# Input tiles and weight blocks in a fixed alternating order at the start of a hybrid decoder kernel

## The chip, the cores and the metric

The kernel runs on all eight cores of one Trainium2 chip. Each core has TensorE (matmuls), ScalarE (ACT), VectorE (DVE), GpSimd (POOL), SyncE (SP) and 16 DMA engines; the page gives each DMA queue's share of them (39.3% and 14.4% for the two large queues of the kernel before). Cores 0 to 3 are die 0 and cores 4 to 7 are die 1. The metric is the device time of the slowest core, in microseconds (us). Executions come in a fast and a slow state (four of the kernel before in one set took 781.88, 781.89, 782.39 and 916.83 us); only fast ones are compared by time here, or the cores of an undisturbed die. A ratio is the mean time of one kernel's fast runs over that of the other kernel's fast runs of the same rounds, so it is not quite the ratio of the medians that are quoted beside it.

## The reference, cut to what matters

```python
u = rmsnorm(x, norm_g)                 # 2048 prompt rows and 16 sample rows a core, 1024 wide
proj = u @ w_in                        # 1024 x 8704: cut into 68 weight blocks of 128 columns
lx, lg, sb, scg, sh, sg, q, qg, mg = split(proj)
# branch A: conv(lx) -> RG-LRU gates -> scan over time, times silu(lg), @ lru_wo
# branch B: conv(scg * sh) * sb * silu(sg), @ sconv_wo
# branch C: softmax(q k^T) v * silu(qg), @ xa_wo; k, v = rmsnorm(mem) @ xa_wk, xa_wv
y = (sigmoid(mg_a) * z_a + sigmoid(mg_b) * z_b + sigmoid(mg_c) * z_c) @ w_out
return rmsnorm(x + y)                  # and the new states; inputs and outputs are float32
```

## The kernel before

The program describes tasks and lets a list scheduler put them in order at build time. The scheduler holds a simple model of every engine and of the DMA queues; it decides nothing on the chip. What it fixes is the order of instructions in each engine's queue. At run time semaphores make an engine wait where data are not there (TensorE 9.3 us for `w_in` in 20:70 us of the kernel before, core 0), and the traces show the queues served in their order: in the kernel before ACT stood 10.6 us before one eviction with the squares of three tiles behind it. **If data come later than the model thought, an engine stands before the one instruction that waits, with ready work behind it.**

```python
# in Graph.run: the model that plans the order
for r, t in lst:
    if r <= m + 0.4:                       # choose by priority among what starts this soon
        k = t.prio
...
if t.dma is not None:
    q, o = ("sw", "hw") if t.eng == "pool" else ("hw", "sw")
    a, n = max(dmafree[q], end + 0.8), t.dma[1] / 250e3      # bytes at 250 GB/s
    both = min(2 * n, max(0.0, dmafree[o] - a))
    dmafree[q] = a + n + both / 2
    fin = dmafree[q] + 1.3
```

The input phase takes 17 tiles of up to 128 rows (512 KB each): load on the SP queue, sum of squares on ACT, reciprocal root on POOL, scaling on DVE or POOL, eight transposes on TensorE, a copy with the norm weights on DVE. Two memory tiles follow, then the state of the samples (`sin`), which is loaded into space that the squares use before.

```python
def p0(ti, src, nr, dst, gcols, tdst, prio):
    x_, xn_, ps = Handle(xring), Handle(xnring), Handle(PS)      # xring: 9 buffers
    G.dma("sp", [(lambda: x_.ap[0:nr, :], src)], nr * 4096, [], [x_.tok], prio, None)
    G.act(... AF.Square ... accum_out=stat ...)
    rstd(ti, nr, prio)
    ... scale; G.pe([tr(kc) for kc in range(KC)], ...); G.dve(... mult by gcols ...)

def wload(ap, prio):                        # one block: 256 KB in bfloat16, on the POOL queue
    ...
    if state["nw"] >= 2:
        G.after(t, t_rs[min(16, state["nw"] + 1)])     # only an order in the plan

def unit(lhs, nk, rhs, u, reads, prio, hold=()):    # 688 columns, two PSUM banks of 344
    ps = Handle(PS)
    ...
    G.pe([mm(k, b) for k in range(nk) for b in range(2)], ...)   # 16 matmuls 128x344

for hd in range(4):
    step(heads_q, hd)
step(branch_A_lg, 0); step(branch_B_sg, 0); step(branch_A_lx, 0)
kv(pos)                                     # memory K/V
for n in range(NCH + 1):                    # 6 chunks of branches A and B
    ...
    if n < 4:
        step(attend, n, d=14)
```

The softmax here doesn't subtract the row's maximum and nothing guards it: scores larger than these inputs give would overflow.

## Time and profile before

| | |
|---|---|
| time | 781.89 us median of 3 (781.88 to 916.83; the last is slow) |
| cores of the profiled run | 776.0 to 782.0 us, mean 778.1 |
| TensorE busy | 726.6 us, 93% of the span |
| TensorE idle in 0:70 us | 30.4 us |

The page's picture in 40 slices (19.5 us each) of the kernel before: a digit is the busy share in tenths; the second row is the clock that TensorE was granted.

```profile
PE   2579998999999998999999999999999999999995
...
PEclk9979998999999999999999999999999999999998
```

TensorE is the engine that sets the time, and more than half of its idle time (30.4 of 55.4 us) lies in the first 70 us. The table by stretches of core 0 shows where; the columns are the stretch, its length, then busy us and instructions of PE, PEld, DVE, ACT and POOL, then granted clock, DMA share and GB/s.

```profile
35.00:40.00 5.00, 0.00 (x0) 0.00 (x0) 1.54 (x3) 1.39 (x3) 3.56 (x6) 0.79 1.12 266
40.00:45.00 5.00, 2.87 (x11) 1.51 (x12) 0.00 (x0) 0.00 (x0) 0.00 (x0) 0.50 1.28 119
```

The timeline of TensorE, same kernel and core (start, length, what, idle time before it and its releaser), and the waits of TensorE in 20:70, name what it stood before:

```profile
24.49 4.03 PE L761 MATMUL PP<-R 128*128 128x344 bf16 x16 [1.48 <-DVE R L674]
28.36 1.50 PE L671 MATMUL PP<-R 128*128 128x128 bf16 x24
29.70 0.23 PE L627 MATMUL PP<-R 66*128 66x66 f32 x1
32.03 2.49 PE L761 MATMUL PP<-R 128*128 128x344 bf16 x16 [2.11 <-DMA R<-w_in]
34.36 0.61 PE L671 MATMUL PP<-R 128*128 128x128 bf16 x8
42.13 4.75 PE L761 MATMUL PP<-R 128*128 128x344 bf16 x16 [7.16 <-DMA R<-w_in]
```

```profile
PE PP L761 <- DMA R<-w_in: 9.3, 2, 7.2
```

A projection unit (16 matmuls) takes 2.33 us back to back later, and 4.03 and 4.75 us in the first and third unit above: most of their matmuls start 287 ns apart, where 146 ns is the interval of the later units, at a granted clock of 1.00 (60:70 us); it is called full speed here. (The granted-clock column shows only the second of these slow stretches: it reads 0.50 in 40:45, but 1.00 in 20:30, where the matmuls are 287 ns apart as well. So in this trace a 1.00 in that column at the start does not prove full speed.) The second weight block is used at 32 us and the third at 42, though the first two were issued at 2 us. Meanwhile ACT stood 10.6 us before one instruction, the eviction of the unit that waits for the third block, with the squares of three tiles behind it:

```profile
46.97 0.73 ACT L936 CAST R<-PP 128x688 bf16<-128x688 f32 x1 [10.57 <-PE PP L761]
47.59 1.06 ACT L659 ACTIVATE R<-R 128x1024 bf16<-128x1024 f32 x1
```

**A measure used below: lost TensorE time.** At a time t it is t minus the full-clock time of all matmuls started by then. Full-clock times are the start-to-start intervals that the trace shows, 146 ns for 344 columns, 216 ns for 512 and 56 ns for 128. The count runs over every TensorE record of a core, and the figures are means of the eight cores. (Two cores in each trace lack 16 to 20 of 4884 matmul records, none of them before 100 us; such a core lacks 3.5 to 4.3 us of work in the whole sum, in all kernels nearly alike. The 36 small transposes of the sample state are counted at about 100 ns each, where the trace shows 61; so all figures after them are some 1.4 us too low, in all kernels alike. They run before 70 us in `before`, e4, g1 and, in most cores, g2, and later elsewhere, so the 70 us column compares these with the others only to within 1.4 us.) Only differences between kernels are used. It takes idle gaps and slow clock together and tells at which time they came.

### The profile page before, as it was taken

The numbers are of one execution on the slowest core, as the hardware profiler recorded it, in microseconds if no ns is written. First come the engines' busy times: TensorE is split into PE (matmuls) and PEld (weight loads), VectorE is DVE, ScalarE is ACT, GpSimd is POOL, SyncE is SP. The second block draws the span as 40 slices with busy tenths as digits, with TensorE's granted clock in tenths as the row PEclk, the third lists the DMA queues.
The fourth block names the chain that finished last, engine by engine and source line by source line (L and its number), as shares of the span: only waits on it lengthen the run. The fifth ranks groups of instructions, "written<-read, shape, count | busy, mean of one in ns | idle before, by whom it ended". The sixth has DMA issues, their size and how long they took to land.

```text
span 782.0 us, 13246 instructions; the slowest of 8 cores (776.0 to 782.0 us)
## 1 busy us (share of the span) xinstructions
PE 726.6 (93%) x4884; PEld 460.6 (59%) x4884; DVE 395.2 (51%) x379; ACT 340.2 (44%) x404; POOL 247.5 (32%) x303
## 2 busy tenths in 40 slices
PE   2579998999999998999999999999999999999995
PEld 1356654655655654666666666666666666665442
DVE  3544043265684863877875874546321221223665
ACT  4442358886759658676571211121212112112332
POOL 5845000121120210212114344435464454423221
PEclk9979998999999999999999999999999999999998
DMA  8999921414242333242334595655896828226933
GB/s 223 296 92 129 117 68 15 41 15 41 28 45 25 28 34 35 28 41 24 39 31 78 81 194 88 94 110 66 111 121 73 119 28 76 23 109 215 294 141 138
DMA packets 112618, 69.47 MB, mean 89 GB/s; under 512 B 93987, under 2 KB 100213, under 8 KB 112539
## 3 DMA queue, kind: packets, MB, share of 16 engines
q0 software_dynamic: 99808, 31.60, 39.3%
q1 hardware_dynamic: 12747, 37.03, 14.4%
q8 instruction: 40, 0.66, 0.4%
q14 instruction: 23, 0.19, 0.1%
HBM read 90.53 MB, written 9.82 MB: 128 GB/s over the span
## 4 chain that ended last, share of the span: by engine, by line
PE 85%; DMA 5%; issue 2%; ACT 2%; DVE 2%; POOL 2%; SPq 0%; POOLq 0%; ACTq 0%; DVEq 0%
PE PP L761 73%; PE PP L1189 8%; DMA R<-w_in 3%; PE PP L967 2%; DMA R<-xp 1%; PE PP L901 1%; ACT R L825 1%; PE PP L959 1%; DMA R<-cv 1%; POOL R L653 1%; PE PP L1053 1%; DVE R L839 1%; ACT R L962 1%; POOL R L663 0%; DVE R L1072 0%
## 5 line engine op out<-in xcount | busy, mean ns | idle before, releaser
L761 PE MATMUL PP<-R 128*128 128x344 bf16 x4104 | 616.5, 311 | 17.2 <-DMA R<-w_in 9.3
L761 PEld LDWEIGHTS PP<-R 128*128 128x128 bf16 x4104 | 400.1, 98 | 225.9 <-issue 28.2
L133 POOL DMA_DIRECT2D R<-w_in x68 | 61.7, 910 | 293.0 <-PE PP L761 266.3
L1141 ACT ACTIVATE R<-PP 128x688 f32<-128x688 f32 x72 | 53.6, 744 | 221.8 <-PE PP L761 197.8
L1150 DVE SCALAR_TENSOR_TENSOR R<-R,PP 128x688 f32<-128x688 f32 x72 | 62.5, 871 | 157.3 <-PE PP L761 134.5
L1189 PE MATMUL PP<-R 128*128 128x512 bf16 (+1 forms) x272 | 59.0, 379 | 0.0
L1154 POOL TENSOR_TENSOR R<-R 128x688 f32<-128x688 f32 x24 | 39.3, 1642 | 33.5 <-DVE R L1150 32.5
L812 DVE SCALAR_TENSOR_TENSOR R<-R 128x2048 f32<-128x2048 f32 x18 | 42.3, 2349 | 8.1 <-ACT R L809 7.0
L1189 PEld LDWEIGHTS PP<-R 128*128 128x128 bf16 (+1 forms) x272 | 26.4, 97 | 32.2 <-issue 0.4
L1159 POOL TENSOR_TENSOR R<-R 128x688 bf16<-128x688 f32 x24 | 38.9, 1642 | 17.7 <-DVE R L1150 17.5
L1198 ACT ACTIVATE R<-R 128x1024 f32<-128x1024 f32 (+1 forms) x17 | 18.0, 1057 | 46.3 <-DVE R L1193 46.3
L867 DVE TENSOR_TENSOR R<-PP,R 128x688 f32<-128x688 f32 x18 | 15.7, 874 | 31.0 <-PE PP L761 31.0
L1193 DVE SCALAR_TENSOR_TENSOR R<-PP,R 128x1024 f32<-128x1024 f32 (+1 forms) x17 | 20.8, 1224 | 20.6 <-PE PP L1189 20.6
L825 ACT ACTIVATE R<-PP,R 128x688 f32<-128x688 f32 x36 | 27.7, 833 | 6.4 <-PE PP L761 6.4
L674 DVE TENSOR_TENSOR R<-PP,R 128x1024 bf16<-128x1024 bf16 (+1 forms) x19 | 21.6, 1171 | 17.0 <-PE PP L671 16.5
L671 PE MATMUL PP<-R 128*128 128x128 bf16 (+1 forms) x152 | 13.7, 252 | 16.5 <-DVE R L663 12.7
L873 DVE SCALAR_TENSOR_TENSOR R<-R 128x2048 f32<-128x2048 f32 x12 | 28.2, 2347 | 0.9 <-ACT R L870 0.7
L651 POOL TENSOR_SCALAR R<-R 128x1 f32<-128x1 f32 (+1 forms) x36 | 7.5, 209 | 62.5 <-ACT R L1198 44.5
L839 DVE TENSOR_TENSOR_SCAN R<-R 128x2048 f32<-128x2048 f32 x6 | 26.5, 4422 | 0.4
L975 DVE TENSOR_TENSOR R<-PP,R 128x512 f32<-128x512 f32 x16 | 10.9, 688 | 29.3 <-ACT R L973 21.4
L1055 DVE TENSOR_TENSOR R<-R,PP 128x1024 f32<-128x1024 f32 x16 | 19.5, 1216 | 11.2 <-PE PP L1053 9.4
L936 ACT CAST R<-PP 128x688 bf16<-128x688 f32 x12 | 8.8, 730 | 35.1 <-PE PP L761 33.5
(129 smaller groups left out, 587.9 us busy)
## 6 DMA issues: line engine op xcount, KB each, us to landing
R<-w_in POOLq DMA_DIRECT2D x68, 256.0 KB, 5.1
R<-xp SPq DMA_DIRECT2D x32, 512.0 KB, 9.1
R<-ck SPq DMA_DIRECT2D x16, 512.0 KB, 4.2
y_p<-R SPq DMA_DIRECT2D x16, 512.0 KB, 2.8
R<-cv POOLq DMA_DIRECT2D x16, 256.0 KB, 7.2
R<-w_out POOLq DMA_DIRECT2D x8, 256.0 KB, 6.4
R<-xa_wo POOLq DMA_DIRECT2D x14, 128.0 KB, 4.1
R<-lru_wo POOLq DMA_DIRECT2D x8, 192.0 KB, 4.6
```

The source lines that it names most:

```text
L133: eng.dma_start(out=out, in_=in_).then_inc(sems[semkey], 16)
L674: G.dve(lambda e: e.tensor_tensor(out=dst, in0=ps.ap.bitcast(BF16)[:, 0:1024].rearrange("p (k t) -> p k t", k=KC)[:, :, 0:nr], in1=gcols.u ...
L761: return lambda e: e.matmul(ps.ap[:, b * 512:b * 512 + BLK], lhs(k), rhs[:, k, c:c + BLK], start=(k == 0), stop=(k == nk - 1))
L812: G.dve(lambda e, k=k: e.scalar_tensor_tensor(out=xc[:, 0:T], in0=lxp[:, k:k + T], scalar=cw(k), in1=xc[:, 0:T], op0=ALU.mult, op1=ALU.add ...
L825: G.act(lambda e, ps=ps, dst=dst, u=u, bcol=bcol: e.activation(out=cols(dst, u), in_=pv(ps), func=AF.Tanh, scale=0.5, bias=dv[:, bcol:bcol ...
L839: G.dve(lambda e: e.tensor_tensor_scan(out=xc[:, 0:T], data0=thr[:, 0:T], data1=thi[:, 0:T], initial=0.0, op0=ALU.mult, op1=ALU.add), T, t ...
L873: G.dve(lambda e, k=k: e.scalar_tensor_tensor(out=cy[:, 0:T], in0=cinp[:, k:k + T], scalar=sw(k), in1=cy[:, 0:T], op0=ALU.mult, op1=ALU.ad ...
L1141: G.act(lambda e, ps=pg[u], th_=th_: e.activation(out=b3(th_.ap), in_=pv(ps), func=AF.Tanh, scale=0.5), UW, [pg[u].tok], [th_.tok], Px - E ...
L1150: G.dve(lambda e, zp=zp, th_=th_, dst=dst: e.scalar_tensor_tensor(out=b3(dst.ap), in0=b3(th_.ap), scalar=1.0, in1=pv(zp), op0=ALU.add, op1 ...
L1154: G.pool(lambda e, acc=acc, th_=th_: e.tensor_tensor(out=acc.ap, in0=acc.ap, in1=th_.ap, op=ALU.add), 1.6, [acc.tok, th_.tok], [acc.tok], Px)
L1159: G.pool(lambda e, acc=acc, th_=th_, u=u, j=j: e.tensor_tensor(out=mT[:, j, u * UW:(u + 1) * UW], in0=acc.ap, in1=th_.ap, op=ALU.add), 1.6 ...
L1189: return lambda e: e.matmul(ps.ap[0:nr, b * 512:(b + 1) * 512], mT[:, k, c0:c0 + nr], wo[:, k, b * 512:(b + 1) * 512], start=(k == 0), sto ...
```

## The change

Intent: each input tile from the seventh on (tile 6) waits for a weight block to land, so that blocks are no longer late behind a crowd of tiles (in the kernel before, core 0, block 1 was issued at 3.1 us and landed at 31.8, and 13 tiles landed in between); 13 blocks are requested in a fixed order, from the third on each after a tile's statistics; the two memory tiles wait for the last of them. The first units are split into two bank halves, the first of which needs only its own tiles. K/V goes behind the first chunk's gates and attention one chunk later. The scheduler's window of choice shrinks from 0.4 to 0.2 us. Cut to its core:

```diff
-                    if r <= m + 0.4:
+                    if r <= m + 0.2:
...
+            if split:
+                for b in range(2):
+                    c = u * UW + b * BLK
+                    t = G.pe([mm(k, b) for k in range(nk)], ..., own tiles of this half, ...)
+                    t.xgate = [t_tr[i] for i in range(17) if i * 128 < (u + 1) * UW] if b == 0 else []
...
+        first = [C_Q, C_Q + 128, C_Q + 256, C_Q + 384, C_LG, C_SG, C_LX, C_SB, C_LG + 128, C_SCG, C_SH, C_SG + 128, C_LX + 128]
+        pre, x_toks, w_toks = {}, [], []
         for i in range(17):
+            if i >= 6:
+                wait = [w_toks[min(i - 5, len(w_toks) - 1)]]
+            elif i >= 3:
+                wait = [x_toks[i - 3]]
+            else:
+                wait = []
...
+            x_toks.append(p0(i, src, nr, uT[...], pT[:, 0:8], t_uT[i], -100 + i, wait))
+            while len(w_toks) < len(first) and len(w_toks) <= max(1, i):
+                hw, lhs = wload(w_in_cols(first[len(w_toks)]), -100 + i)
+                ...
+                    G.after(G.tasks[-1], t_rs[i])
...
-        kv(pos)
-        pos += 10
         for n in range(NCH + 1):
...
-            if n < 4:
-                step(attend, n, d=14)
+            if n == 0:
+                kv(pos)
+                pos += 10
+            if 1 <= n < 5:
+                step(attend, n - 1, d=14)
```

(`xgate` makes the planner start a unit only after the transposes of all its tiles have been placed.)

More of the change, by code (lines that the diff above doesn't have):

```diff
@@ L181 @@
 class Task:
-    __slots__ = ("i", "eng", "dur", "fns", "reads", "writes", "prio", "hs", "tset", "npred", "succ", "pf", "dma", "preds", "start", "gate", "etset")
+    __slots__ = ("i", "eng", "dur", "fns", "reads", "writes", "prio", "hs", "tset", "npred", "succ", "pf", "dma", "preds", "start", "gate", "etset", "xgate")
 EXP = frozenset((0, 6))
@@ L248, in _add @@
         t.start = None
+        t.xgate = []
         for p in preds:
@@ L295, in _gates @@
         for t in self.tasks:
-            t.gate = []
+            t.gate = list(t.xgate)
             t.etset = None
@@ L358, in run @@
             if best is None:
-                stuck = [(t.eng, t.i, [k.name for k in t.writes], [h.ring.name for h in t.hs if h.phys is None])
-                         for c in ready.values() for t in c]
-                held = {}
-                for t in self.tasks:
-                    for h in t.hs:
-                        if h.phys is not None and h.left > 0 and t.start is None:
-                            held.setdefault((h.ring.name, h.phys), []).append((t.eng, t.i, t.prio, [k.name for k in t.reads], [k.name for k in t.writes],
-                                [(p.i, p.eng, [k.name for k in p.writes]) for p in t.preds if p.start is None][:4]))
-                raise RuntimeError(f"no task can start: {stuck[:8]} held {held}")
+                stuck = [(t.eng, t.i, [k.name for k in t.writes]) for c in ready.values() for t in c]
+                raise RuntimeError(f"no task can start: {stuck[:8]}")
             _, start, t = best
@@ L413, in run @@
                 if sem is None:
-                    h = t.hs[0]
+                    h = (t.writes or t.reads)[0].handle
                     sem = h.ring.sem + str(h.phys)
@@ L628, in params, with wload, w_in_cols, unit @@
             G.dve(lambda e: e.tensor_copy(pT[:, 16:82], h.ap[:, 0:66]), 66, [h.tok], [m_pT.t], -86)
+        def wload(ap, prio):
+            k = ap.shape[1]
+            hw = Handle(w2ring if 2 <= state["nw"] < 6 else wring)
+            G.dma("pool", [(lambda: hw.ap[:, 0:k * 128].rearrange("p (k c) -> p k c", k=k), ap)], k * 65536 * 1.18, [], [hw.tok], prio, None)
+            state["nw"] += 1
+            if "pre" in state:
+                G.after(G.tasks[-1], state["pre"])
+            return hw, (lambda i: hw.ap[:, i * 128:(i + 1) * 128])
+        def w_in_cols(c0):
+            return w_in.rearrange("(k p) c -> p k c", p=128)[:, :, c0:c0 + 128]
+        def unit(lhs, nk, rhs, u, reads, prio, hold=(), split=False):
+            ps = Handle(PS)
+            def mm(k, b):
+                c = u * UW + b * BLK
+                return lambda e: e.matmul(ps.ap[:, b * 512:b * 512 + BLK], lhs(k), rhs[:, k, c:c + BLK],
+                                          start=(k == 0), stop=(k == nk - 1))
+            if split:
+                for b in range(2):
+                    c = u * UW + b * BLK
+                    t = G.pe([mm(k, b) for k in range(nk)], nk * 0.1465, [r for r in reads if r not in t_uT] + utoks(c, c + BLK), [ps.tok],
+                             prio + 0.1 * b)
+                    t.xgate = [t_tr[i] for i in range(17) if i * 128 < (u + 1) * UW] if b == 0 else []
+            else:
+                G.pe([mm(k, b) for k in range(nk) for b in range(2)], nk * 2 * 0.1465, reads, [ps.tok], prio, hold)
+            return ps
+        def pv(ps, n=BLK):
+            return ps.ap.rearrange("p (b c) -> p b c", b=2)[:, :, 0:n]
+        def cols(arr2d, u, off=0):
+            return arr2d[:, off + u * UW: off + (u + 1) * UW].rearrange("p (b c) -> p b c", b=2)
+        def usl(u):
+            return utoks(u * UW, (u + 1) * UW)
+        def proj(c0, prio, lead=30.0, hold=((), (), ())):
+            hw, lhs = pre.pop(c0) if c0 in pre else wload(w_in_cols(c0), prio - lead)
+            return [unit(lhs, KC, uT, u, [hw.tok] + usl(u), prio + 2.4 * u, hold[u], prio < 60) for u in range(NU)]
         m_xb = [side(f"xb{i}", i * 4096, 1024, F32) for i in range(5)]
@@ L645, in build_program @@
         t_st = [m_stat.tok(f"st{i}") for i in range(40)]
-        t_rs = []
+        t_rs, t_tr = [], []
         def rstd(col, nr, prio):
@@ L654, in rstd, with p0 @@
                                [t_st[col], m_cst.t], [t_st[col]], prio))
-        def p0(ti, src, nr, dst, gcols, tdst, prio):
+        def p0(ti, src, nr, dst, gcols, tdst, prio, wait):
             x_, xn_, ps = Handle(xring), Handle(xnring), Handle(PS)
-            G.dma("sp", [(lambda: x_.ap[0:nr, :], src)], nr * 4096, [], [x_.tok], prio, None)
+            G.dma("sp", [(lambda: x_.ap[0:nr, :], src)], nr * 4096, wait, [x_.tok], prio, None)
             G.act(lambda e: e.activation(out=m_junk.ap[0:nr, :], in_=x_.ap[0:nr, :], func=AF.Square,
@@ L672, in tr @@
                                              xn_.ap[0:nr, kc * 128:(kc + 1) * 128], identb[0:nr, 0:nr])
-            G.pe([tr(kc) for kc in range(KC)], 0.65, [xn_.tok, m_identb.t], [ps.tok], prio)
+            t_tr.append(G.pe([tr(kc) for kc in range(KC)], 0.65, [xn_.tok, m_identb.t], [ps.tok], prio))
             G.dve(lambda e: e.tensor_tensor(
@@ L677, in p0 @@
                 [ps.tok, t_pg], [tdst], prio)
+            return x_.tok
+        first = [C_Q, C_Q + 128, C_Q + 256, C_Q + 384, C_LG, C_SG, C_LX, C_SB, C_LG + 128, C_SCG, C_SH, C_SG + 128, C_LX + 128]
+        pre, x_toks, w_toks = {}, [], []
         for i in range(17):
+            if i >= 6:
+                wait = [w_toks[min(i - 5, len(w_toks) - 1)]]
+            elif i >= 3:
+                wait = [x_toks[i - 3]]
+            else:
+                wait = []
             nr = 128 if i < 16 else TS
             src = xp[i * 128:(i + 1) * 128, :] if i < 16 else xs[:, :]
-            p0(i, src, nr, uT[:, :, i * 128:i * 128 + nr], pT[:, 0:8], t_uT[i], -100 + i)
+            x_toks.append(p0(i, src, nr, uT[:, :, i * 128:i * 128 + nr], pT[:, 0:8], t_uT[i], -100 + i, wait))
+            while len(w_toks) < len(first) and len(w_toks) <= max(1, i):
+                hw, lhs = wload(w_in_cols(first[len(w_toks)]), -100 + i)
+                pre[first[len(w_toks)]] = hw, lhs
+                if len(w_toks) >= 2:
+                    G.after(G.tasks[-1], t_rs[i])
+                w_toks.append(hw.tok)
+                last = G.tasks[-1]
+        state["pre"] = last
         for i in range(2):
-            p0(17 + i, memp[i * 128:(i + 1) * 128, :], 128, mnT[:, :, i * 128:(i + 1) * 128], pT[:, 8:16], t_mn[i], -80 + i)
+            p0(17 + i, memp[i * 128:(i + 1) * 128, :], 128, mnT[:, :, i * 128:(i + 1) * 128], pT[:, 8:16], t_mn[i], -80 + i, w_toks[-1:])
         params()
@@ L741, in build_program @@
               [m_pT.t, m_dv.t], [m_dv.t], -84)
-        def wload(ap, prio):
-            k = ap.shape[1]
-            hw = Handle(w2ring if 2 <= state["nw"] < 6 else wring)
-            t = G.dma("pool", [(lambda: hw.ap[:, 0:k * 128].rearrange("p (k c) -> p k c", k=k), ap)], k * 65536 * 1.18, [], [hw.tok], prio, None)
-            if state["nw"] >= 2:
-                G.after(t, t_rs[min(16, state["nw"] + 1)])
-            state["nw"] += 1
-            return hw, (lambda i: hw.ap[:, i * 128:(i + 1) * 128])
-        def w_in_cols(c0):
-            return w_in.rearrange("(k p) c -> p k c", p=128)[:, :, c0:c0 + 128]
-        def unit(lhs, nk, rhs, u, reads, prio, hold=()):
-            ps = Handle(PS)
-            def mm(k, b):
-                c = u * UW + b * BLK
-                return lambda e: e.matmul(ps.ap[:, b * 512:b * 512 + BLK], lhs(k), rhs[:, k, c:c + BLK],
-                                          start=(k == 0), stop=(k == nk - 1))
-            G.pe([mm(k, b) for k in range(nk) for b in range(2)], nk * 2 * 0.1465, reads, [ps.tok], prio, hold)
-            return ps
-        def pv(ps, n=BLK):
-            return ps.ap.rearrange("p (b c) -> p b c", b=2)[:, :, 0:n]
-        def cols(arr2d, u, off=0):
-            return arr2d[:, off + u * UW: off + (u + 1) * UW].rearrange("p (b c) -> p b c", b=2)
-        def usl(u):
-            return utoks(u * UW, (u + 1) * UW)
-        def proj(c0, prio, lead=30.0, hold=((), (), ())):
-            hw, lhs = wload(w_in_cols(c0), prio - lead)
-            return [unit(lhs, KC, uT, u, [hw.tok] + usl(u), prio + 2.4 * u, hold[u]) for u in range(NU)]
         lxp, xc, xcb, thr, thi, a2 = m_lxp.ap, m_xc.ap, m_xcb.ap, m_thr.ap, m_thi.ap, m_a2.ap
```

## The prediction

> **What bounds the kernel now.** TensorE: the page gives PE 726.6 us busy of 782.0 (93%). Most of its idle time is at the start. The table by stretches shows PE at 39.6 us busy in the first 70 us (30.4 idle), against 12 in 150:700. Part of the early busy time is slow as well: sixteen 128x344 matmuls take 4.03 to 4.75 us at 24 to 47 us and 2.33 us later; the granted clock was 0.50 at 40:45 and 0.69 at 45:50. By the PE timeline, the work done before the memory K/V matmuls start at 100.15 us is 336 projection matmuls (x 146 ns = 49.2 us), 19 tiles of transposes (0.61 each, 11.6) and 3.6 of small ones: 64.4 us. So about 36 us of TensorE are lost by then.
>
> **Why.** The waits name weights: 9.3 us on w_in, 7.2 of it at 35 to 42 us. Two weight blocks are issued at 2 us, the second is used only at 32.0, and a third, issued at 18.2, at 42.1. Meanwhile nine tile buffers fill. The DMA view shows 3.4 KB packets on the input queue and 330 B on the weight queue;[...] tiles landed every 1.95 us, and the second block took 28 us. Then ScalarE and VectorE stand still for 10.6 and 11.0 us behind the late block.
>
> **What the change does.** No arithmetic changes; 21 units split into halves, the same matmuls. Tile 6 and later wait for a weight block. From the stretches, a block moves at about 110 GB/s: 2.4 us; a tile at 290 GB/s: 1.8 us. A pair so costs about 4.2 us. My estimate: tiles 0 to 5 land by 17 us, block 1 by about 20.5, then one pair each 4.2 us: tile 10 at 41, tile 15 at 61, block 12 at 66. TensorE starts units at about 21 to 23 us, is fed at some 70% until tile 10 has passed through square, scale and transpose (5 us, so 46 us) and always busy after: by 46 us about 25 us of work done, 21 lost. With 3 us for cold clock and misplaced orders, 24 lost against 36: a gain of 12 us, all critical. The split saves a copy or two (1.2 us each).
>
> Moving K/V behind the first gates and attention one chunk later takes the poorly filled stretch 117:132 apart (gain 0 to 3), but K/V weights now wait for the gate buffer and block the weight queue (loss 0 to 4). I count zero.
>
> **Prediction.** 770 us, range 760 to 779. Faster by over 2%: 0.27; within 2%: 0.68; slower: 0.05.
>
> **What would show it.** First projection units at 20 to 24 us; no wait over 3 us on w_in before 70; clock near 1 from 30 us; PE idle in 0:70 down from 30 to about 20; the K/V matmuls no longer before the gates.
>
> **What would make it wrong.** Waits tile-on-block adding round trips, so that pairs take over 5 us;[...] the later K/V load stalling the weight queue at 100 to 150 us; or a start gain taken back because the vector chain of the first chunks, not TensorE, sets the pace there.

## The result, and the profile after

The changed kernel took 785.58 us (median of 4, 784.52 to 786.75), the kernel before 782.14 in the same rounds: ratio 1.0045, 95% interval 1.0026 to 1.0065. A second measurement (run `f1_after`) gave 1.001, 0.998 to 1.0039. So it is the same within 2%, and if anything slower. The prediction of 770 was wrong.

The page of the changed kernel, same two rows:

```profile
PE   2678899899999989989999999999989999999995
...
PEclk9999899999999999999999999999999999999998
```

The hole at 35 to 47 us is gone. But the first digits are not much higher in sum, and new dips appear. The table by stretches, core 0:

```profile
25.00:30.00 5.00, 2.40 (x14) 1.75 (x15) 1.28 (x2) 2.33 (x5) 4.18 (x7) 1.00 1.16 203
30.00:35.00 5.00, 5.00 (x39) 3.39 (x37) 1.96 (x2) 1.31 (x2) 3.29 (x5) 1.00 1.28 187
...
55.00:60.00 5.00, 1.29 (x11) 0.64 (x8) 1.23 (x1) 1.48 (x3) 1.87 (x3) 1.00 1.23 220
...
80.00:90.00 10.00, 9.20 (x62) 6.58 (x63) 3.05 (x11) 0.73 (x1) 0.00 (x0) 0.66 0.17 17
```

The timeline of TensorE shows the first unit at 28.4 us (24.5 before), a stop at 56 to 61, and one at 78 to 81:

```profile
27.60 1.01 PE L708 MATMUL PP<-R 128*128 128x128 bf16 x8 [4.20 <-POOL R L700]
28.41 3.57 PE L642 MATMUL PP<-R 128*128 128x344 bf16 x16
...
61.02 0.78 PE L708 MATMUL PP<-R 128*128 128x128 bf16 x8 [4.73 <-ACT R L955]
...
80.80 3.30 PE L767 MATMUL PP<-R 16*128 16x16 f32 x36 [2.42 <-DMA R<-st_sc]
```

No wait names `w_in` any more: the alternating order did what it was made for. The new waits each lead to a queue. The timeline of ACT has squares that wait for tiles, and the eviction that TensorE lacks at 56 to 61 us stands directly behind one (L955 is that eviction, L696 a square):

```profile
23.89 1.06 ACT L696 ACTIVATE R<-R 128x1024 bf16<-128x1024 f32 x1 [5.71 <-DMA R<-xp]
...
59.11 1.06 ACT L696 ACTIVATE R<-R 128x1024 bf16<-128x1024 f32 x1 [3.52 <-DMA R<-xp]
60.07 0.19 ACT L696 ACTIVATION_READ_ACCUMULATOR R<-R 128x1 f32 x1
60.16 0.71 ACT L955 CAST R<-PP 128x688 bf16<-128x688 f32 x1
```

The first of these, at 23.9 us, is tile 5. It should have come right after tile 4 (17.0 us). The waits of the SP queue in 0:24 us show why, together with the queue's instructions in program order:

```profile
SPq L131 <- DMA R<-w_in: 11.2, 2, 8.7
```

```
10 L133 DMACopy R<-xp 128x1024 [waits d_xb0]      tile 3
11 L133 DMACopy R<-xp 128x1024 [waits d_xb1]      tile 4
12 L133 DMACopy R<-xp 128x1024 [waits d_w1]       tile 6, waits for weight block 1
13 L133 DMACopy R<-xp 128x1024 [waits d_xb2]      tile 5, waits for tile 2
14 L133 DMACopy R<-xp 128x1024 [waits d_v0]       tile 7, waits for weight block 2
```

**Tile 6 stands in front of tile 5.** The planner believed that block 1 would land at 10 us, before tile 2, so it placed tile 6 first. On the chip block 1 landed at 17.6 us: the SP queue stood 8.7 us before tile 6, with tile 5 behind it, ready to go from 11.3 us, when tile 2 had landed, and the first unit needs tiles 0 to 5.

The lost TensorE time, mean of the eight cores (us at that time):

| | at 40 | 50 | 70 | 100 | 350 | 600 | range over cores at 100 |
|---|---|---|---|---|---|---|---|
| before | 30.6 | 34.3 | 37.8 | 39.1 | 55.5 | 60.9 | 38.3 to 39.9 |
| after | 27.8 | 29.6 | 35.5 | 37.4 | 53.6 | 60.5 | 33.2 to 41.9 |

At 50 us the changed kernel is 4.7 us ahead; at 100 us 1.7 are left, at 600 us 0.4. And the cores differ more. The core listing of both kernels (span, mean granted clock), three cores of each, before and then after:

```profile
core 0: 782.0 us, clock 0.983
...
core 2: 776.0 us, clock 0.992
...
core 5: 776.3 us, clock 0.990
```

```profile
core 0: 784.0 us, clock 0.985
...
core 2: 771.9 us, clock 0.992
...
core 5: 768.7 us, clock 0.996
```

The mean core took 778.1 us before and 776.9 after in these two executions (over all fast runs of the set of `f1_after`: 777.8 and 775.5), so the mean improved by 1.2 to 2.3 us, while the slowest, which is the metric, did not. The three slowest cores at the end (0, 6 and 1) are among the four that had lost most by 100 us (41.9, 39.0 and 40.5 us; core 3 had lost 39.7).

### The profile page after: what moved, and what is told of

It reads as the page before. It is cut to its first block, busy times and chain, and to the rows that moved or that the text cites. A ratio compares the mean times of both kernels' runs of the same rounds, so it can differ in the third digit from the quotient of the medians.

```text
span 784.0 us, 13244 instructions; the slowest of 8 cores (768.7 to 784.0 us)
## 1 busy us (share of the span) xinstructions
PE 726.4 (93%) x4865; PEld 460.9 (59%) x4884; DVE 397.5 (51%) x379; ACT 333.8 (43%) x400; POOL 249.3 (32%) x303
## 3 DMA queue, kind: packets, MB, share of 16 engines
q0 software_dynamic: 99808, 31.60, 39.7%
q1 hardware_dynamic: 12747, 37.03, 14.5%
## 4 chain that ended last, share of the span: by engine, by line
PE 80%; DMA 9%; ACT 4%; issue 3%; DVE 1%; POOL 1%; SPq 0%; POOLq 0%; ACTq 0%; DVEq 0%
PE PP L642 67%; PE PP L1209 7%; DMA R<-xp 4%; DMA R<-w_in 2%; DMA R<-xa_wk 2%; PE PP L986 2%; DMA R<-st_sc 1%; ACT R L844 1%; PE PP L920 1%; DMA R<-cv 1%; PE PP L1073 1%; PE PP L978 1%; PE PP L767 0%; PE PP L1112 0%; ACT R L696 0%
## 5 line engine op out<-in xcount | busy, mean ns | idle before, releaser
L1161 ACT ACTIVATE R<-PP 128x688 f32<-128x688 f32 x72 | 53.6, 744 | 226.6 <-PE PP L642 204.2
L1174 POOL TENSOR_TENSOR R<-R 128x688 f32<-128x688 f32 x24 | 39.3, 1643 | 34.7 <-DVE R L1170 33.5
L1209 PEld LDWEIGHTS PP<-R 128*128 128x128 bf16 (+1 forms) x272 | 26.4, 97 | 32.2 <-issue 0.4
L696 ACT ACTIVATE R<-R 128x1024 bf16<-128x1024 f32 (+1 forms) x19 | 20.1, 1056 | 24.6 <-DMA R<-xp 24.3
L708 PEld LDWEIGHTS PP<-R 128*128 128x128 bf16 (+1 forms) x152 | 11.4, 113 | 30.2 <-issue 29.5
L892 DVE SCALAR_TENSOR_TENSOR R<-R 128x2048 f32<-128x2048 f32 x12 | 28.2, 2347 | 0.2
L844 ACT ACTIVATE R<-PP,R 128x688 f32<-128x688 f32 x36 | 27.7, 834 | 0.9 <-PE PP L642 0.7
L858 DVE TENSOR_TENSOR_SCAN R<-R 128x2048 f32<-128x2048 f32 x6 | 26.5, 4417 | 0.1
L1075 DVE TENSOR_TENSOR R<-R,PP 128x1024 f32<-128x1024 f32 x16 | 19.5, 1217 | 12.4 <-PE PP L1073 11.0
L886 DVE TENSOR_TENSOR R<-PP,R 128x688 f32<-128x688 f32 x18 | 15.7, 872 | 16.4 <-PE PP L642 16.1
```

What stands on the lines that cost most here:

```text
L708: return lambda e: e.transpose(ps.ap.bitcast(BF16)[:, kc * 128:kc * 128 + nr], xn_.ap[0:nr, kc * 128:(kc + 1) * 128], identb[0:nr, 0:nr])
L844: G.act(lambda e, ps=ps, dst=dst, u=u, bcol=bcol: e.activation(out=cols(dst, u), in_=pv(ps), func=AF.Tanh, scale=0.5, bias=dv[:, bcol:bcol ...
L858: G.dve(lambda e: e.tensor_tensor_scan(out=xc[:, 0:T], data0=thr[:, 0:T], data1=thi[:, 0:T], initial=0.0, op0=ALU.mult, op1=ALU.add), T, t ...
L892: G.dve(lambda e, k=k: e.scalar_tensor_tensor(out=cy[:, 0:T], in0=cinp[:, k:k + T], scalar=sw(k), in1=cy[:, 0:T], op0=ALU.mult, op1=ALU.ad ...
L1161: G.act(lambda e, ps=pg[u], th_=th_: e.activation(out=b3(th_.ap), in_=pv(ps), func=AF.Tanh, scale=0.5), UW, [pg[u].tok], [th_.tok], Px - E ...
L1174: G.pool(lambda e, acc=acc, th_=th_: e.tensor_tensor(out=acc.ap, in0=acc.ap, in1=th_.ap, op=ALU.add), 1.6, [acc.tok, th_.tok], [acc.tok], Px)
```

## The experiments

Theory A: the early gain is real but is lost to queue orders planned for arrival times that do not hold. Rival B: the move of K/V and attention ate it. Rival C: transfers alone set the pace of the start. Rival D: the chunk stage sets the end whatever the start. All runs gave correct results. The first set (the runs named e) fell into the slow state (die 1 at a mean clock of 0.96 to 0.98 in the profiled executions), so from that set only lost time up to 100 us and the cores of die 0 are used, and no ratio is given; all later sets ran fast but for single slow executions, which are left out, two of the sets on the same chip as the first.

| run | median us (before, same set) | ratio, 95% | first unit, mean | lost at 40 | 70 | 100 | 350 | 600 |
|---|---|---|---|---|---|---|---|---|
| before | 781.89 | | 24.6 | 30.6 | 37.8 | 39.1 | 55.5 | 60.9 |
| after | 785.58 (782.14) | 1.0045, 1.0026 to 1.0065 | 29.0 | 27.8 | 35.5 | 37.4 | 53.6 | 60.5 |
| e1_tile5 | 794.18, slow (800.50) | | 24.6 | 25.6 | 33.0 | 35.6 | | |
| e2_kvback | 805.20, slow (800.50) | | 28.8 | 27.5 | 35.6 | 38.0 | | |
| e3_tile5_plan | 791.69, slow (800.50) | | 24.5 | 24.6 | 26.5 | 27.5 | | |
| e4_before_kv | 803.22, slow (800.50) | | 24.7 | 30.6 | 37.8 | 39.0 | | |
| f1_after | 783.40 (782.46) | 1.0010, 0.9980 to 1.0039 | 28.8 | 27.6 | 35.3 | 37.3 | 52.9 | 59.3 |
| f2_tile5_plan | 776.06 (782.46) | 0.9930, 0.9906 to 0.9955 | 24.8 | 23.9 | 25.6 | 26.7 | 44.9 | 52.5 |
| f3_plan_only | 779.99 (782.46) | 0.9966, 0.9946 to 0.9986 | 28.5 | 27.4 | 29.3 | 31.1 | 50.0 | 57.8 |
| f4_tile5_plan_nosplit | 775.75 (782.46) | 0.9916, 0.9899 to 0.9933 | 26.5 | 25.5 | 26.5 | 27.1 | 46.0 | 53.0 |
| g1_before_plan | 783.52 (781.83) | 1.0017, 0.9993 to 1.0041 | 27.6 | 27.4 | 39.0 | 39.7 | 56.8 | 61.9 |
| g2_after_nowait | 782.92 (781.83) | 1.0014, 0.9982 to 1.0047 | 24.0 | 29.9 | 33.7 | 35.3 | 51.6 | 58.9 |
| g3_after_look04 | 788.98 (781.83) | 1.0077, 1.0048 to 1.0105 | 29.3 | 28.1 | 37.9 | 42.7 | 60.7 | 67.2 |
| g4_tile5_plan_mem | 777.01 (781.83) | 0.9925, 0.9895 to 0.9956 | 24.8 | 24.4 | 26.3 | 27.7 | 47.6 | 54.9 |
| h1_before_plan_state | 776.93 (781.40) | 0.9939, 0.9915 to 0.9964 | 27.5 | 27.2 | 33.8 | 33.3 | 50.5 | 55.7 |
| h2_nowait_plan_state | 777.99 (781.40) | 0.9949, 0.9923 to 0.9975 | 23.9 | 28.9 | 33.5 | 33.4 | 49.2 | 55.7 |
| h3_tile5_plan | 774.49 (781.40) | 0.9917, 0.9886 to 0.9949 | 24.8 | 24.0 | 25.8 | 26.6 | 44.9 | 52.4 |

### e1_tile5: put tile 5 in front of tile 6

```diff
-                wait = [w_toks[min(i - 5, len(w_toks) - 1)]]
+                wait = [w_toks[min(i - 5, len(w_toks) - 1)]] + ([x_toks[3]] if i == 6 else [])
```

The added wait was expected to cost nothing on the chip (in `after`, core 0, tile 3 landed at 15.3 us and block 1 at 17.6); it makes the planner place tile 6 later.

> The changed kernel, but tile 6 waits for tile 3 as well, so that its transfer is issued after that of tile 5 (in the changed kernel the SyncE queue held tile 6, which waits 8.7 us for weight block 1, in front of tile 5). Theory A (the early gain was lost to this inversion and then to queues ordered for tiles that come later than planned): tile 5 is squared at about 18 us, not 23.9, first projection unit at 22 to 24 us, not 28.4; lost TensorE time at 46 us falls from 28 to about 23; part of that is given back at 50 to 100 us, so the time falls by 2 to 6 us against the changed kernel. Rival B (the K/V and attention move took the gain back): less than 1.5 us changes. Rival C (the transfer rate alone sets the pace of the first 60 us): first units earlier, but lost time at 60 us the same.

Tile 5 was squared at 18.7 us (mean of the cores) in place of 24.5, and the first unit ran at 24.6 in place of 29.0, as theory A and C had it. At 40 us 2.2 us less were lost than in the changed kernel, at 50 nothing (29.8 against 29.6), at 100 us 1.8 less. Theory A had put the loss at 46 us at about 23; it was 28.2 there, so that number missed. So the inversion is real, but alone it buys little: at 40 to 50 us the next misplaced instruction takes most of it back (`f2_tile5_plan` below shows that it is a matter of order). Rival B, which expected no change, is not supported; C is neither shown nor refuted by this run.

### e2_kvback and e4_before_kv: the K/V move alone, both ways

```diff
 # e2: the changed kernel            # e4: the kernel before, the opposite edit
+        kv(pos)
+        pos += 10
         for n in range(NCH + 1):
...
-            if n == 0:
-                kv(pos)
-                pos += 10
-            if 1 <= n < 5:
-                step(attend, n - 1, d=14)
+            if n < 4:
+                step(attend, n, d=14)
```

> The changed kernel with the K/V block and the attention steps back at their old places, alternating order kept. Rival B: 8 us or more faster than the changed kernel, near 775. Theory A: within 3 us of the changed kernel, as the lost TensorE time between 100 and 350 us was equal before and after (16.4 and 16.2 us); lost time at 70 us unchanged.

> The kernel before with only the K/V block and attention moved as in the change. Rival B: 5 to 10 us slower than the kernel before. Theory A: within 3 us of it; lost TensorE time at 70 us as before (37.8).

With the old place, the changed kernel lost 37.9 us by 100 us on die 0 and 63.8 by 400, that is 25.9 us in between; the changed kernel as it is lost 16.8 there and the kernel before 17.2 (54.2 minus 37.4, 56.3 minus 39.1). The four cores of die 0 took 782.7 to 790.2 us. So undoing the move did not help; it cost some 9 us, which theory A had put at 3 at most, so that number missed. In the kernel before, the move cost about 2 us between 100 and 400 (19.5 against 17.2, die 0). Rival B expected 8 us of gain from the first and 5 to 10 us of loss from the second; it falls.

### e3_tile5_plan, f2_tile5_plan: also plan for the tiles' real arrival

The planner assumed a tile and a block every 3.05 us (tile 7 at 27.0 us, tile 15 at 51.3 in its own log); on core 0 tiles 7 and 15 were squared at 28.5 and 63.0 us, 4.3 us apart each. So the rate in its model is lowered in that stretch. No arithmetic and no explicit wait changes. (The planner also hands out the ring buffers in the order that it plans, so which earlier use of a buffer a load or an operation waits for can change with it; no run separates this from the order.)

```diff
-                a, n = max(dmafree[q], end + 0.8), t.dma[1] / 250e3
+                a, n = max(dmafree[q], end + 0.8), t.dma[1] / (185e3 if 15 < start < 70 else 250e3)
```

> As the first run of this set, and the transfer rate that the kernel's own list scheduler assumes is lowered from 250 to 185 GB/s between 15 and 70 us of its plan, so that it plans the last tiles for about 60 us, where they were seen, and not for 51. No wait is removed; only the order in the engines' queues changes. Theory A: the waits of TensorE at 56 to 61 us and of ScalarE for tiles while evictions stand behind (3.5 and 2.7 us) shrink; lost TensorE time at 100 us falls by 3 to 6 us below that of the first run; time 3 to 6 us below it. Rival B and C: no change over 2 us.

> Tile 5 ahead of tile 6 and the slower transfer rate in the kernel's own plan, as in run e3_tile5_plan, to be timed beside the control in the same state. Theory A: lost time at 100 us 27 to 28 us, 9 to 10 below the control; some 3 us of it given back at 100 to 350 us; time 6 to 9 us below the control, 0.6 to 1.1% faster than the kernel before. If the early gain does not reach the end (rival D: the chunk stage at 100 to 350 us sets the end whatever the start), within 3 us of the control.

> The changed kernel as it is, as the control for the other runs of this set on the same chip: 0.2 to 0.7% slower than the kernel before; lost TensorE time about 37 us at 100 us, first projection unit at 28 us.

Lost time at 100 us fell to 27.5, 26.7 and 26.6 us in the three runs of this kernel (`h3_tile5_plan` is the third), against 37.3 and 37.4 in the changed kernel. The timeline of TensorE of `f2_tile5_plan`, core 0, has no gap over 0.7 us between 26 and 100 us, where the changed kernel had gaps of 4.7 and 2.4; here is the stretch around 56 to 61 us:

```profile
54.41 0.61 PE L708 MATMUL PP<-R 128*128 128x128 bf16 x8 [0.65 <-DVE R L700]
54.85 3.66 PE L642 MATMUL PP<-R 128*128 128x344 bf16 x24
58.35 0.61 PE L708 MATMUL PP<-R 128*128 128x128 bf16 x8
58.80 2.50 PE L642 MATMUL PP<-R 128*128 128x344 bf16 x16
61.21 0.61 PE L708 MATMUL PP<-R 128*128 128x128 bf16 x8
61.65 2.50 PE L642 MATMUL PP<-R 128*128 128x344 bf16 x16
```

The time fell to 776.06 us beside 783.40 for the changed kernel and 782.46 for the kernel before. The fall from e1 to e3, 8.1 us at 100 us, was larger than the 3 to 6 expected. Transfers were only a little faster at their end: tile 15 landed at 59.2 us (mean of the cores) and in the control `f1_after` at 62.2. In `f3_plan_only` below it landed at 61.0, and 6.2 us less were lost than in the control. So rival C falls as well, most clearly by f3: 1.2 us in arrival go with 6.2 us in loss. Rival D expected the end to stay; of the 10.6 us at 100 us, 8.0 are left at 350 and 6.8 at 600, so it explains a part and not the whole.

### f3_plan_only: fit the plan, leave tile 5 behind tile 6

> The changed kernel with only the slower transfer rate in its plan; tile 5 still stands behind tile 6. Theory A: first unit still at 28 us, lost time at 40 us still 27 to 28; but the growth from 50 to 100 us (7.8 us in the changed kernel) falls under 4, so lost time at 100 us is 31 to 34. If the 50:100 loss came from late transfers and not from queue order, the growth stays at 7 or more.

As expected: the first unit stayed at 28.5 us, and the loss between 50 and 100 us fell from 7.8 us to 2.3 (28.8 to 31.1). With f2 this splits the 10.6 us at 100 us: 6.2 belong to orders planned for tiles that were expected too early, 4.4 to tile 5 behind tile 6. The split depends on which is mended first: with tile 5 first (e1, then e3) it is 1.8 and 8.1. Either way the planned order is the larger part.

### f4_tile5_plan_nosplit: without the split by bank

```diff
-            return [unit(..., hold[u], prio < 60) for u in range(NU)]
+            return [unit(..., hold[u]) for u in range(NU)]
```

> As f2_tile5_plan without the split of the first units by bank. The first unit then waits for the copies of tiles 3 to 5 as well: first unit 1 to 2.5 us later than 24 us, lost time at 100 us 0 to 2 us more than in f2_tile5_plan; time within 3 us of it.

The first unit came 1.7 us later, and at 100 us 0.4 us more were lost. The time is the same (775.75 and 776.06). The split saves at the very start what it was meant to, and nothing of it reaches the end.

### g3_after_look04: the scheduler's window of choice

```diff
-                    if r <= m + 0.2:
+                    if r <= m + 0.4:
```

> The changed kernel with the scheduler's lookahead back at 0.4. No theory makes it a cause: first unit at 28 us, lost time at 100 us within 2.5 us of the changed kernel (37.3), time within 4 us of it.

This expectation missed. The window alone costs 5.4 us of lost time at 100 us (42.7 against 37.3) and the kernel is 0.8% slower than before. Nothing but the planner's choices (the order in the queues, and the ring buffers with it) differs, so it agrees with theory A in kind: in this phase the order alone is worth 5 us and more either way.

### g2_after_nowait: the change without its waits

```diff
-                wait = [w_toks[min(i - 5, len(w_toks) - 1)]]
...
-                wait = [x_toks[i - 3]]
+                wait = []                     # in all cases, memory tiles too
```

> The changed kernel without the waits of tiles for blocks (all input tiles free to go, as before), with the new block order, split, lookahead and K/V place. Theory A: block 1 lands at 28 to 32 us again, the order is planned for earlier blocks, lost time at 100 us 36 to 41 us, time within 5 us of the changed kernel. If alternation as such is worth much, it is over 5 us slower than the changed kernel.

Block 1 was late again: the profile has a wait of TensorE on `w_in` of 5.4 us before 38.8.

```profile
38.82 2.45 PE L642 MATMUL PP<-R 128*128 128x344 bf16 x8 [5.38 <-DMA R<-w_in]
```

Yet lost time at 100 us was 35.3, two less than with the waits and just under the 36 to 41 expected, and the time was the same. As the change stands, its central part buys nothing.

### g1_before_plan, then h1 and h2: is the alternation worth anything with orders that fit?

g1 gives the kernel before a plan that knows how late its blocks come, and leaves the transfers as they are:

```diff
-                a, n = max(dmafree[q], end + 0.8), t.dma[1] / 250e3
-                both = min(2 * n, max(0.0, dmafree[o] - a))
+                a, n = max(dmafree[q], end + 0.8), t.dma[1] / (48e3 if q == "sw" and start < 19 else 250e3)
+                both = 0.0 if start < 45 else min(2 * n, max(0.0, dmafree[o] - a))
```

> The kernel before, no alternation, with only the transfer times of its own plan set to what its trace shows: weight blocks 0 to 2 at 48 GB/s (planned landings 22, 30, 42 us; seen at about 24, 32, 42) and tiles unhindered by them. Only queue orders change. Theory A: the loss from 35 to 50 us was ScalarE and TensorE queued behind a block that the plan had promised for 26 us and that came at 42; now lost time at 100 us is 30 to 34 us instead of 39.1, and the time falls 4 to 8 us below the kernel before. If the weights' late arrival itself were the loss (then only alternation could mend it), lost time at 100 us stays at 37 or more.

The number missed, for a reason of the same kind. At 50 us 3.5 us less were lost than before (30.8 against 34.3) and the wait on `w_in` was gone; but the transposes of the sample state (L712) now stood at 54 us, before that state had come, and the clock fell to half in all cores around 51 to 71 us:

```profile
62.37 3.99 PE L712 MATMUL PP<-R 16*128 16x16 f32 x36 [8.21 <-DMA R<-st_sc]
```

h1 is g1 with the planned transfer of that state lengthened (planned bytes 300,000 to 4,500,000, nothing moved on the chip), h2 is g2 with both corrections, and h3 is the alternating kernel of f2 as a control.

> The kernel before with its plan fitted to seen weight landings, as in g1_before_plan, and the planned transfer of the sample state lengthened, so that its transposes are put at 67 us and not at 49. No wait removed, no alternation. Theory A (order, not arrival, was the loss): the 8.2 us wait at 54 to 62 us is gone, lost TensorE time at 100 us 31 to 34 us (39.1 before), time 4 to 8 us below the kernel before. If a further misplaced piece appears, or arrival itself is the loss, lost time stays at 37 or more.

> The changed kernel without the waits of tiles for blocks, with both plan corrections of h1. If alternation as such is worth nothing, lost time at 100 us is within 2 us of h3 (26.7) ; if alternation gains by feeding blocks earlier, it is 3 us or more above it, 30 to 34. I expect the second, as blocks 1 and 2 land at about 30 and 39 us without it and at 18 and 24 with it.

> The control: the same kernel as f2_tile5_plan. Lost time at 100 us 26 to 28 us; 0.5 to 1.0% faster than the kernel before.

Without alternation 33.3 and 33.4 us are lost at 100 us, with it 26.6. **Fitting the order to the kernel before, without any of the change, recovers 5.8 us (39.1 to 33.3); the alternating kernel with a fitted order loses 6.7 us less again.** How much of the 6.7 is alternation alone is not shown. h1 also lacks the change's window, split and K/V place. h2 has them, but its plan does not fit: its planner promises blocks 3 to 12 for 55 to 88 us, and on core 0 they landed at 43 to 64. (The slow rate copied from h1 falls on every block issued before 19 us of the plan, and h2 issues more of them by then.) The first block that came earlier than planned is block 2 (38.8 us, mean; planned 42.4). At 37 us, before that can matter, h2 had already lost 27.9 us and h3 24.0. So 3.9 us go with the late blocks before the misfit sets in, and the rest stays open.

In time, h1 has a ratio of 0.9939 and h3 of 0.9917; their intervals overlap. The mean of the eight cores varies less than the slowest: it was 772.1 to 773.6 us in the four executions of h1, 772.0 to 773.8 in those of h2, and 768.8 to 770.1 in those of h3. So the kernel with alternation is the faster one by some 3 us, with the same open question of what in it does that.

### g4_tile5_plan_mem: memory tiles one block earlier

```diff
-            p0(17 + i, ..., t_mn[i], -80 + i, w_toks[-1:])
+            p0(17 + i, ..., t_mn[i], -80 + i, w_toks[11:12])
```

> As f2_tile5_plan, with the memory tiles waiting for block 11 in place of block 12, so that they, and the sample state behind them, come about 4 us earlier. In f2_tile5_plan five of eight cores still have one stretch of half clock at 81 to 84 us. Theory A: that stretch disappears in most cores, lost time at 100 us 0 to 1.5 us below f2_tile5_plan, time 0 to 3 us below it.

A miss. The half-clock stretch that starts at 81 to 84 us in five cores of f2 starts at 76 to 79 in seven cores here; it did not vanish, and nothing was gained (27.7 us lost at 100, ratio 0.9925 against 0.9930 for f2).

## Why the prediction was wrong, point by point

- **"TensorE bounds, and about 36 us are lost by 100 us" held.** The finer count gives 39.1, as it takes a tile's eight transposes at 0.45 us and not at 0.61.
- **"The second block took 28 us" held:** 28.7 us, issued at 3.1 and landed at 31.8 (core 0). In 10:18 us, while both queues moved data, the DMA view of the kernel before (packets, MB, share) counts nearly the same number of packets on the input queue (q1) and on the weight queue (q0):

```profile
q1 hardware_dynamic: 587, 2.13, 84.4%
q0 software_dynamic: 589, 0.15, 20.2%
```

  An estimate from these lines: a block of 256 KB is about 1,000 packets of 0.25 KB; at one for one, 1,000 packets of the input queue, at 3.6 KB, are some seven tiles. With tiles free to go, block 1 was used at 32.0 us; with tiles 0 to 4 ahead of it and the rest held back, it landed at 17.6. But I took lateness to be the loss. In h1 the blocks come as late as before (core 0: blocks 1 and 2 landed at 32.9 and 41.4 us, before at 31.8 and 41.7) and 5.8 of the 39.1 us are gone: part of the loss was the order behind a promise of 26 us for block 2 (first used at 42).
- **"A pair so costs about 4.2 us" held:** 4.3 us between tiles 7 and 15. "Block 1 by about 20.5" came earlier, 17.6.
- **"Tiles 0 to 5 land by 17 us" failed first.** Tile 5 was squared at 24.5 (mean), because the SP queue held tile 6 in front of it. The step "TensorE starts units at about 21 to 23 us" became 29.0. I had read the dependence of tile 6 on block 1 as a matter of that tile alone; in a queue it is a matter of everything behind it, and which tile is behind is settled by the planner's model. With the order mended, the first unit ran at 24.6 to 24.8.
- **"And always busy after" failed second.** The loss from 50 to 100 us was 7.8 us where I had allowed 3 for all. Squares of tiles (10 to 15) that were planned 7 to 12 us too early stood in ACT's queue in front of evictions, and transposes in TensorE's queue in front of ready units. f3 takes 5.5 us of the 7.8 away by order alone. I wrote of "misplaced orders" and gave them a share of 3 us with the cold clock; they cost 10.6 us at 100 us (f1 against f2), tile 5 included. This is the larger of the two failed steps: mended alone, the plan gives back 6.2 us at 100 us (f3) and tile 5 1.8 (e1).
- **The size of what could be had was right:** "24 lost against 36, a gain of 12"; with fitted orders the loss at 100 us is 12.4 and 12.5 us below that of the kernel before (26.7 and 26.6 against 39.1).
- **"A gain of 12 us, all critical" was too much.** Of 12.4 at 100 us, 8.4 are left at 600 (60.9 minus 52.5) and 6.4 in the time (782.46 minus 776.06). Between 100 and 350 us f2 loses 18.2 us, the kernel before 16.4. The waits there name ACT and DVE results, as before (core 0, the longest two: 3.3 us for DVE and 3.2 for ACT in e3, the same kernel; 3.2 and 3.3 in the kernel before). That an earlier start runs into the pace of the vector chain is argued, not shown; no run took a vector operation away.
- **K/V counted as zero:** between 100 and 350 us the loss is 16.4 before and 16.2 after, so the sum held. The parts did not: e2 shows that the old place costs the changed kernel some 9 us.
- **The mean and the slowest core:** I predicted one core. At 100 us the cores of the kernel before lie within 1.6 us and those of the changed kernel within 8.7 us. In f2 the range is 25.3 to 28.2. Part of the spread is clock: in the profiled execution of the changed kernel core 0 had 17.1 us at half clock between 35 and 740 us and core 5 none; an estimate from that, half of 17.1, is 8.5 of the 15.3 us between their spans (784.0 and 768.7). That waits which hang on which transfer wins spread the cores is argued; no run isolates it.
- Not explained: the changed kernel loses 6.9 us between 350 and 600 us, the kernel before 5.4. A wait for sample values grew from 1.3 to 2.1 us and a half-clock stretch at 570 to 580 us shows in some cores. This was not tested.

A version better than both is h3/f2 (0.9917 and 0.9930), and without the split f4 (0.9916): the alternation with tile 5 in its place and a plan that knows the transfer rate. It stays under 2%.

## What to carry to other kernels

Where a build-time scheduler orders queues that are served in order, as the SP queue was here (8.7 us before tile 6, with tile 5 behind it), a change of transfers is only worth what its new arrival times are known: compare planned and measured arrival of each tile first, and correct the model before judging the change. When a wait is added to one entry of a queue, list what stands behind it in that queue; the price is paid there. On eight cores read the spread, not one core: a change can help the mean and leave the slowest where it was.

## The queues and the clock, as measured here

- One waiting DMA held back a ready one behind it in the same queue: in the changed kernel, core 0, the SP queue stood 8.7 us before tile 6, and tile 5, whose own wait had ended at 11.3 us, was issued at 18.1. The first matmul unit came 4.4 us later than with tile 5 in front (29.0 against 24.6).
- The second 256 KB block took 28.7 us to land in the kernel before (issued at 3.1, landed at 31.8, core 0), at 0.25 KB a packet beside an input queue of 3.6 KB packets (both in 10:18 us), and 14.5 us in the changed kernel, where of the input tiles only 0 to 4 ran beside it.
- The half-clock stretches of the profiled executions of the kernel before and the changed kernel, all cores, before 740 us, are 3.4, 6.8 and 10.2 us long. In the changed kernel, core 0, one of 6.8 us began at 81.8 us, after a gap of 2.4 us (78.4 to 80.8) and one microsecond of the 36 small transposes. What starts such a stretch was not shown.
- In the fast runs all eight cores kept a mean granted clock of 0.979 to 0.998, with TensorE 93% busy in the kernel before, and the records of both kernels' profiled executions hold no share but 1.0 and 0.5. In one slow execution of the kernel before (914.46 us) die 1 had a mean of 0.81 to 0.84. The same chip ran two later sets fast but for single executions, of which this was one.
